# The seven products of each pair of tiles of the branch projections, pair by pair

## The chip, the cores and the metric

The kernel runs on one core of one Trainium2 chip. The metric is device microseconds (us) of one execution, as the median of three timed runs. One more execution was taken with the hardware profiler; its rows are what this document reads. Engines in these rows: PE is TensorE's matmul, PEld its weight load, DVE is VectorE, ACT is ScalarE, POOL is GpSimd, and SP is SyncE, whose queue (SPq) issues the DMA transfers here.

## The reference

One inference step of a decoder layer (DEPTH is 1) on 1024 prompt rows and 8 single samples, D_MODEL 1024, branch width 512, all in fp32. The part that the change touches is the merge of three branches by gates:

```python
h = _rmsnorm(x, norm_g) * (1 + scale) + shift
p = h @ w_in
...                                     # y_a, y_b, y_c: three branches, each (T, 512)
merged = (jax.nn.sigmoid(m_a) * (y_a @ w_branch[0])
          + jax.nn.sigmoid(m_b) * (y_b @ w_branch[1])
          + jax.nn.sigmoid(m_c) * (y_c @ w_branch[2]))
x = x + gate * (merged @ w_out)
```

`w_branch[b]` is 512 x 1024. So each branch projection is a product of 1024 x 512 weights with 512 x 1032 data, multiplied element by element by a gate and added to the other two.

## The kernel before

**Data.** Data lie transposed: features on the 128 partitions, the 1032 columns (1024 rows and 8 samples) along the free axis, in two halves of H = 516, each in two parts of HC = 258 columns, which is the width of a matmul. A fp32 product is made of three matmuls on numbers split in a high and a low part: high weights by high data (L1120), high weights by low data (L1121), low weights by high data (L1122). The split of a block is two instructions: ScalarE makes the high part (L109), VectorE the low one as the difference (L110). High parts have names with h (`yh0T4`), low ones with l (`yl0T4`).

**Seven products a pair.** The projection of a branch has eight tiles of 128 output features. Two tiles `m0`, `m1` form a pair and are computed together by a scheme with seven block products in place of eight (a variant of Strassen's): the weights come as A11, A12, A22 (in `pw..a`, high and low half) and sums S1 to S4 (in `pw..s`), the data as blocks B11, B21, B22 and sums T1 to T4. The sums of the weights were made earlier and lie in HBM, as do the gates (`sd`, after ScalarE's sigmoid, stored by L991 and L992) and the branches (`yd`). A product is 12 matmuls of 128x258 (two parts of columns, two blocks of 128 rows, three matmuls each). Branches come in the order 1, 0, 2 (`n` = 0, 1, 2), four pairs each: p10 to p13, p00 to p03, p20 to p23. The list `flat` holds these 12 pairs. The seven products of a pair, and what follows each:

```python
"P1": J(mm("B1", "A11", "B11", True, False), seed, dma, a=WD),
"P5": J(mm("B5", "S1", "T1", True, False), snap("B5", "p5")),
"P2": J(mm("B2", "A12", "B21", False, True), lambda: gated(m0, 0, "B2"), s_dma, r=-1.0, a=SD),
"P6": J(mm("B1", "S2", "T2", False, False), snap("B1", "u2")),
"P3": J(mm("B5", "S4", "B22", False, True), right, r=0.0),
"P7": J(mm("B1", "S3", "T3", False, False), lambda: added(m1, "B1", "p5", False), r=0.0),
"P4": J(mm("B1", "A22", "T4", False, True), last, r=-1.0),
```

P1 writes bank B1. The *seed* (ScalarE, L1140) copies B1 to bank B2, where P2 adds its product; P6, P7 and P4 add theirs to B1. The *snaps* (ScalarE, L1134) copy P5's bank and, after P6, B1 to an array `pu`. VectorE adds P3's bank to one half of `pu` and multiplies by the gate of m0 (`right`: L1150 twice, L1153), after P7 the same for m1; *gated* (L1145, two instructions) multiplies P2's bank by m0's gate, and P4's by m1's. So the first half of columns of m0 comes from P2, that of m1 from P4. After P4, `summed` (L1159) adds m0 and m1 to the sums of the branches before (for n of 1 and 2).

**The planner.** Each product is a `Job`; the jobs run in the order in which they were made, and this fixes the order of instructions on every engine. A job's `dma` goes out as soon as the job is nearer than its lead, counted in the planned durations (1.45 us for a product) of the jobs between: WD = 16 us for the weights of a pair (at P1, L1099), SD = 8 us for its two gates (at P2, L1104). Within that, transfers are issued on SyncE in the order of the jobs that triggered them, between whatever else SyncE has to issue, and SyncE's queue takes its rows one after the other. Work that may come later is put in a list `behind` (`later`), and each job takes from it: a product with positive room (P1, P5, P6: 1.0) right after its matmuls and ahead of its own copies, one with negative room (P2, P4: -1.0) behind its own, and P3 and P7 take none. The splits of the *next* branch's blocks, and the sums T1 to T4 (L1062) that they need, are put in that list by the table NEXT: the entry `(3, "P6"): "T4"` says that when P6 of the branch's last pair (number 3) is made, the split of T4 for the next branch goes on the list. `"dma"` loads the next branch's data (L1056, eight transfers, `yr`).

**The order.** `go` makes one product's job. Each pair runs P5, P2, P6, P3, P7, then P1 of the *next* pair, then its own P4; the very last pair has P5, P6, P3, P7, P2, P4.

Of the kernel before, what the change touches and what calls it, by code (L numbers as in the profile page):

```python
# [56 lines left out]

RM = 1.0

NEXT = {(1, "P2"): "dma", (1, "P4"): "B11", (1, "P3"): "T1+", (2, "P5"): "T1", (2, "P2"): "B21 T3+", (2, "P6"): "T2+ T4+",  # L60
        (3, "P5"): "T2 B22", (3, "P2"): "T3", (3, "P6"): "T4"}

LAST = {(1, 2): "dma", (1, 4): "B11", (1, 5): "T1+", (1, 6): "T1", (0, 0): "B21", (0, 1): "T3+", (0, 2): "T2+", (0, 3): "T4+",
        (0, 4): "T2", (0, 5): "B22", (0, 6): "T3", (0, 7): "T4"}
# [10 lines left out]
def hybrid_step_kernel(ctx: ExitStack, tc: tile.TileContext, ins, outs):  # L75
# [1177 lines left out]
    flat = [(n, i, t) for n in range(3) for i, t in enumerate(branches[n])]  # L1253

    def go(j, x):
        n, i, t = flat[j]
        t[x]()
        if n < 2 and (i, x) in NEXT:
            hooks[n + 1](NEXT[i, x])

    go(0, "P1")
    for j in range(len(flat)):
        for x in ("P5", "P2", "P6", "P3", "P7") if j + 1 < len(flat) else ("P5", "P6", "P3", "P7", "P2"):
            go(j, x)
        if j + 1 < len(flat):
            go(j + 1, "P1")
        go(j, "P4")


    wo_h, wo_l, xr, oacc = {}, {}, {}, {}  # L1270
# [265 lines left out]
```

## Time and profile before

| | |
|---|---|
| median of 3 runs | 903.98 us (903.88 to 906.06) |
| the profiled execution | 906.72 us, of which the span (first to last instruction) is 905.0 us |
| granted TensorE clock, mean of the span | 0.995 of full speed |
| TensorE busy | 890.9 us, 98% |
| VectorE, ScalarE, GpSimd busy | 625.0, 398.5, 30.4 us |
| moved by DMA | 152.96 MB, 169 GB/s on average |

The sum of what happens is set by the engine that is always busy, here TensorE. A busy share is an average over the program's stages: the stretch that this change touches runs from about 674.8 us (first product of p10) to 797.1 us (end of p23), and is read by itself below. The rows give a start and a duration in us, the engine, the line, and what was written from what; "idle before <-" names what an engine waited for. A line number is that of the kernel before.

### The profile page before, as it was taken

The page shows a single profiled execution, that of the slowest core. Times are in us where ns is not written, and L with a number is a line of the kernel's source. Part 1 is how long each engine was busy: PE and PEld are TensorE (multiplying, and loading weights), DVE is VectorE, ACT ScalarE, POOL GpSimd, SP SyncE. Part 2 cuts the span into 40 slices and gives each one's busy share as a digit, 9 for nine tenths or more (in the row PEclk, how much of TensorE's full clock was granted, in tenths as well). Part 3 has the DMA queues.
Part 4 walks back from the last instruction along what each step waited for, and adds up shares of the span by engine and source line. Part 5 has one row for each costly group of instructions (what it writes and reads, how often), then busy time and mean ns, then how long its engine had stood idle before and what let it go on. Part 6 is the DMA issues. An engine that isn't in the chain of part 4 may idle for free.

```text
span 905.0 us, 17515 instructions
## 1 busy us (share of the span) xinstructions
PE 890.9 (98%) x7126; PEld 864.2 (95%) x7126; DVE 625.0 (69%) x1149; ACT 398.5 (44%) x743; POOL 30.4 (3%) x72
## 2 busy tenths in 40 slices
PE   8999999999999999999999999999999999999996
PEld 8677999999999999999999999999999999999995
DVE  4676758667877667866756667578565889893634
ACT  5666572454444334335544544445453433451211
POOL 1450000000000000000000000000000000000001
PEclk9999999999999999999999999999999999999998
DMA  8905213225746263440721614606579999570103
GB/s 314 353 1 152 76 67 86 83 90 211 255 166 231 94 221 117 177 152 13 281 82 71 245 47 141 222 1 234 188 276 388 385 338 347 206 255 1 49 23 118
DMA packets 65185, 152.96 MB, mean 169 GB/s; under 512 B 12232, under 2 KB 23240, under 8 KB 65104
## 3 DMA queue, kind: packets, MB, share of 16 engines
q1 hardware_dynamic: 65104, 151.83, 47.0%
q8 instruction: 56, 0.92, 0.4%
q14 instruction: 25, 0.20, 0.1%
HBM read 105.95 MB, written 45.86 MB: 168 GB/s over the span
## 4 chain that ended last, share of the span: by engine, by line
PE 90%; DVE 1%; ACT 1%; issue 0%; DVEq 0%
PE o L1287 3%; PE o L1288 3%; PE o L1289 3%; PE g_2B L575 2%; PE g_1B L577 2%; PE g_2B L577 2%; PE g_0B L577 2%; PE g_3B L577 2%; PE g_0B L578 2%; PE g_2B L578 2%; PE g_1B L575 2%; PE g_0B L575 2%; PE g_1B L578 2%; PE g_3B L578 2%; PE g_3B L575 2%; PE u0B L575 1%
## 5 line engine op out<-in xcount | busy, mean ns | idle before, releaser
L1287 PE MATMUL o<-mh,woh 128*128 128x388 f32 (+1 forms) x192 | 62.2, 324 | 0.0
L1288 PE MATMUL o<-ml,woh 128*128 128x388 f32 (+1 forms) x192 | 61.5, 320 | 0.0
L1289 PE MATMUL o<-mh,wol 128*128 128x388 f32 (+1 forms) x192 | 61.3, 319 | 0.0
L1288 PEld LDWEIGHTS o<-ml,woh 128*128 128x128 f32 x192 | 36.1, 188 | 0.3
L1287 PEld LDWEIGHTS o<-mh,woh 128*128 128x128 f32 x192 | 36.1, 188 | 0.3
L1289 PEld LDWEIGHTS o<-mh,wol 128*128 128x128 f32 x192 | 36.2, 188 | 0.0
L1391 ACT ACTIVATE osq<-xr 128x388 f32<-128x388 f32 (+1 forms) x21 | 10.3, 492 | 48.5 <-DVE xr L1380 28.1
L375 PE MATMUL v<-bvw,hhi 128*128 128x512 f32 x64 | 26.4, 413 | 0.2 <-ACT hhi L292 0.2
L377 PE MATMUL v<-bvw,hlo 128*128 128x512 f32 x64 | 25.5, 398 | 0.7 <-DVE hlo L296 0.7
L376 PE MATMUL v<-bvw,hhi 128*128 128x512 f32 x64 | 25.2, 394 | 0.0
L1377 DVE SCALAR_TENSOR_TENSOR xr<-o,gt,xr 128x384 f32<-128x384 f32 x16 | 9.8, 614 | 19.9 <-PE o L1289 19.8
L323 PE MATMUL warm<-ones 128*128 128x128 f32 x158 | 21.4, 300 | 1.1 <-DVE ones L130 1.1
L323 PEld LDWEIGHTS warm<-ones 128*128 128x128 f32 x158 | 20.6, 214 | 1.9 <-DVE ones L130 1.1
L577 PE MATMUL g_1B<-hlo,g_1wB 128*128 128x258 f32 x72 | 20.4, 283 | 0.0
L575 PE MATMUL g_1B<-hhi,g_1wB 128*128 128x258 f32 x72 | 20.4, 283 | 0.0
L575 PE MATMUL g_2B<-t,g_2w 128*128 128x258 f32 x72 | 20.4, 283 | 0.0
L575 PE MATMUL g_2B<-hhi,g_2wB 128*128 128x258 f32 x72 | 20.4, 283 | 0.0
L577 PE MATMUL g_2B<-hlo,g_2wB 128*128 128x258 f32 x72 | 20.4, 283 | 0.0
L577 PE MATMUL g_1B<-t,g_1w 128*128 128x258 f32 x72 | 20.4, 283 | 0.0
L578 PE MATMUL g_1B<-hhi,g_1wB 128*128 128x258 f32 x72 | 20.4, 283 | 0.0
L578 PE MATMUL g_0B<-hhi,g_0wB 128*128 128x258 f32 x72 | 20.4, 283 | 0.0
L578 PE MATMUL g_2B<-hhi,g_2wB 128*128 128x258 f32 x72 | 20.3, 283 | 0.0
(1393 smaller groups left out, 3741.4 us busy)
## 6 DMA issues: line engine op xcount, KB each, us to landing
sig<-sd SPq DMA_DIRECT2D x24, 516.0 KB, 6.5
ada<-in_ada SPq DMA_DIRECT2D x16, 512.0 KB, 8.4
wr<-in_wbr SPq DMA_DIRECT2D x12, 512.0 KB, 5.0
x<-in_xT SPq DMA_DIRECT2D x16, 256.0 KB, 6.2
gr<-in_ada_g SPq DMA_DIRECT2D x8, 512.0 KB, 7.1
wor<-in_wo SPq DMA_DIRECT2D x8, 512.0 KB, 4.9
xr<-in_xf SPq DMA_DIRECT2D x8, 512.0 KB, 5.3
sd<-g_0o SPq DMA_DIRECT2D x6, 516.0 KB, 3.3
```

The costliest lines, as they stand in the source:

```text
L323: PE.matmul(ps[:, :P], lhsT=ones, rhs=ones, start=True, stop=True)
L375: PE.matmul(vacc[i], lhsT=lh, rhs=w[:, 0, :], start=start, stop=False)
L376: PE.matmul(vacc[i], lhsT=lh, rhs=w[:, 1, :], start=False, stop=False)
L377: PE.matmul(vacc[i], lhsT=ll, rhs=w[:, 0, :], start=False, stop=stop)
L575: PE.matmul(o, lhsT=w[:, 0, f_], rhs=bh, start=start and k == 0, stop=False, skip_group_check=True)
L577: PE.matmul(o, lhsT=w[:, 0, f_], rhs=bl, start=False, stop=False, skip_group_check=True)
L578: PE.matmul(o, lhsT=w[:, 1, f_], rhs=bh, start=False, stop=stop and k == KW - 1, skip_group_check=True)
L1287: PE.matmul(o, lhsT=wo_h[k][:, w], rhs=cols(mhi[k]), start=start, stop=False)
L1288: PE.matmul(o, lhsT=wo_h[k][:, w], rhs=cols(mlo[k]), start=False, stop=False)
L1289: PE.matmul(o, lhsT=wo_l[k][:, w], rhs=cols(mhi[k]), start=False, stop=stop)
L1377: V.scalar_tensor_tensor(x[:, :m], ps[:, :m], gt[:, f, 0:1], x[:, :m], ALU.mult, ALU.add)
L1391: A_.activation(o_like(c, sq), x, AF.Square)
```

## The change

Every pair now runs its own seven products P1, P5, P6, P3, P7, P2, P4, in the order that only the last pair ran in nearly the same form before. No product of the next pair comes ahead of P4, and P2 comes as last but one. The table NEXT is written anew with the same tasks in the same order, hooked to the products that now stand in the places: for instance the split of T4 goes on the list at (3, "P2"), which is now the sixth product of the pair.

```diff
-NEXT = {(1, "P2"): "dma", (1, "P4"): "B11", (1, "P3"): "T1+", (2, "P5"): "T1", (2, "P2"): "B21 T3+", (2, "P6"): "T2+ T4+",
-        (3, "P5"): "T2 B22", (3, "P2"): "T3", (3, "P6"): "T4"}
+NEXT = {(1, "P6"): "dma", (1, "P2"): "B11", (1, "P4"): "T1+", (2, "P5"): "T1", (2, "P6"): "B21 T3+", (2, "P2"): "T2+ T4+",
+        (3, "P5"): "T2 B22", (3, "P6"): "T3", (3, "P2"): "T4"}
...
-    go(0, "P1")
     for j in range(len(flat)):
-        for x in ("P5", "P2", "P6", "P3", "P7") if j + 1 < len(flat) else ("P5", "P6", "P3", "P7", "P2"):
+        for x in ("P1", "P5", "P6", "P3", "P7", "P2", "P4"):
             go(j, x)
-        if j + 1 < len(flat):
-            go(j + 1, "P1")
-        go(j, "P4")
```

What stands in a row on two engines, before and after. First SyncE's queue around the first pair, p10, before: `pw10s1` and `pw11..` are weights of the pairs p10 and p11, `sig1_0` and `sig1_1` the gates of p10's two tiles, `sd2_6` and `sd2_7` the stores of the last two gate tiles that the stage before computes.

```order
L1099 DMA pw10s1_7872<-wd10s1_2183 128x1024
L1104 DMA sig1_0_8001<-sd1_0_777 128x1032
L1104 DMA sig1_1_8003<-sd1_1_778 128x1032
L1099 DMA pw11a0_8005<-wd11a0_2445 128x768
L1099 DMA pw11a1_8007<-wd11a1_2447 128x768
L1099 DMA pw11s0_8009<-wd11s0_2435 128x1024
L1099 DMA pw11s1_8011<-wd11s1_2437 128x1024
L991 DMA sd2_6_791<-g2_3o1_7937 128x1032
L992 DMA sd2_7_792<-g2_3o2_7968 128x1032
L1104 DMA sig1_2_8118<-sd1_2_779 128x1032
```

And the same place of SyncE's queue after the change:

```order
L1099 DMA pw10s1_7872<-wd10s1_2183 128x1024
L991 DMA sd2_6_791<-g2_3o1_7937 128x1032
L992 DMA sd2_7_792<-g2_3o2_7968 128x1032
L1104 DMA sig1_0_8035<-sd1_0_777 128x1032
L1104 DMA sig1_1_8037<-sd1_1_778 128x1032
L1099 DMA pw11a0_8039<-wd11a0_2445 128x768
L1099 DMA pw11a1_8041<-wd11a1_2447 128x768
L1099 DMA pw11s0_8043<-wd11s0_2435 128x1024
L1099 DMA pw11s1_8045<-wd11s1_2437 128x1024
L1056 DMA yr0B11_8180<-yd0_0_757 128x516
```

The two stores moved from behind six loads to ahead of them, and the next branch's data (`yr0`) now come right behind `pw11`.

Second, VectorE in the first pair of a following branch, p00, before. `p00B2`, `p00B5` and `p00B1` are the banks (the last digit is the part of columns), `yl0..` the low parts of the blocks of this branch.

```order
L110 TENSOR_TENSOR yl0B22_8597<-yr0B22_8193,yh0B22_8596 128x1032
L1145 TENSOR_TENSOR sig0_0_8504<-p00B20_8560,sig0_0_8504 128x258
L1145 TENSOR_TENSOR sig0_0_8504<-p00B21_8562,sig0_0_8504 128x258
L110 TENSOR_TENSOR yl0T3_8618<-yr0B12_8190,yh0T3_8617 128x1032
L110 TENSOR_TENSOR yl0T4_8634<-yr0B21_8187,yh0T4_8633 128x1032
L1150 TENSOR_TENSOR p00pu_8600<-p00B50_8582,p00pu_8600 128x258
L1150 TENSOR_TENSOR p00pu_8600<-p00B51_8589,p00pu_8600 128x258
L1153 TENSOR_TENSOR sig0_0_8504<-p00pu_8600,sig0_0_8504 128x516
L1150 TENSOR_TENSOR p00pu_8600<-p00B10_8546,p00pu_8600 128x258
L1150 TENSOR_TENSOR p00pu_8600<-p00B11_8553,p00pu_8600 128x258
L1153 TENSOR_TENSOR sig0_1_8506<-p00pu_8600,sig0_1_8506 128x516
L1145 TENSOR_TENSOR sig0_1_8506<-p00B10_8546,sig0_1_8506 128x258
```

The same pair on VectorE after the change:

```order
L110 TENSOR_TENSOR yl0B22_8597<-yr0B22_8189,yh0B22_8596 128x1032
L110 TENSOR_TENSOR yl0T3_8616<-yr0B12_8186,yh0T3_8615 128x1032
L1150 TENSOR_TENSOR p00pu_8600<-p00B50_8582,p00pu_8600 128x258
L1150 TENSOR_TENSOR p00pu_8600<-p00B51_8589,p00pu_8600 128x258
L1153 TENSOR_TENSOR sig0_0_8548<-p00pu_8600,sig0_0_8548 128x516
L1150 TENSOR_TENSOR p00pu_8600<-p00B10_8560,p00pu_8600 128x258
L1150 TENSOR_TENSOR p00pu_8600<-p00B11_8567,p00pu_8600 128x258
L1153 TENSOR_TENSOR sig0_1_8550<-p00pu_8600,sig0_1_8550 128x516
L1145 TENSOR_TENSOR sig0_0_8548<-p00B20_8578,sig0_0_8548 128x258
L1145 TENSOR_TENSOR sig0_0_8548<-p00B21_8580,sig0_0_8548 128x258
L110 TENSOR_TENSOR yl0T4_8666<-yr0B21_8183,yh0T4_8665 128x1032
L1145 TENSOR_TENSOR sig0_1_8550<-p00B10_8560,sig0_1_8550 128x258
```

P2's two multiplications moved from the second place to the last but one, and the low part of T4 moved with them, from ahead of the pair's sums to between P2's multiplications and P4's.

Third, VectorE from the last pair of branch 0, p03, to the first of branch 2, p20, after the change: `sig1_4` and `sig1_5` are the running sums of finished tiles.

```order
L1145 TENSOR_TENSOR sig0_6_8951<-p03B20_8978,sig0_6_8951 128x258
L1145 TENSOR_TENSOR sig0_6_8951<-p03B21_8980,sig0_6_8951 128x258
L1159 TENSOR_TENSOR sig1_4_8297<-sig1_4_8297,sig0_4_8820 128x1032
L1145 TENSOR_TENSOR sig0_7_8953<-p03B10_8963,sig0_7_8953 128x258
L1145 TENSOR_TENSOR sig0_7_8953<-p03B11_8970,sig0_7_8953 128x258
L1159 TENSOR_TENSOR sig1_5_8299<-sig1_5_8299,sig0_5_8822 128x1032
L110 TENSOR_TENSOR yl2T2_9102<-yr2B11_8701,yh2T2_9101 128x1032
L110 TENSOR_TENSOR yl2B22_9124<-yr2B22_8710,yh2B22_9123 128x1032
L110 TENSOR_TENSOR yl2T3_9143<-yr2B12_8707,yh2T3_9142 128x1032
```

Before, P2's multiplications and the sum of `sig1_4` stood ahead of the pair's own additions (L1150, L1153), and only the sum of `sig1_5` and P4's multiplications came between those and the split of T2; now two sums and four multiplications stand in a row ahead of that split.

## Rows read from the trace of the kernel before

**Rows 1.** The head of the page and its first section: the span; for each engine the time in which it was busy, its share of the span, and the number of its instructions.

```profile
span 905.0 us, 17515 instructions
...
PE 890.9 (98%) x7126; PEld 864.2 (95%) x7126; DVE 625.0 (69%) x1149; ACT 398.5 (44%) x743; POOL 30.4 (3%) x72
```

**Rows 2.** The list of TensorE's waits: the waiting instruction's tile and line, what it waited for, then the sum in us, how often, and the longest.

```profile
PE ss L204 <- DVE sq L228: 2.2, 1, 2.2
...
PE p23B L1120 <- DVE p23pu L1150: 0.5, 1, 0.5
PE p10B L1120 <- ACT p10B L1140: 0.3, 1, 0.3
```

**Rows 3.** TensorE's timeline: start and duration in us, then the operation, its tile and its inputs, and idle time before it where there was any (the first matmul of P2 in p10 after the seed; the first matmuls of P1, P5's low weights, P2 in p11; the first of p12; and the first two of P4's data T4, here named with its blocks, in p23). The last row is of the view of one tile, `pw12s`: least, median and largest duration in ns, then the start of the first and of the last of 12.

```profile
678.17 0.39 PE L1120 MATMUL p10B<-yh1B,pw10a 128*128 128x258 f32 x1 [0.33 <-ACT p10B L1140]
...
684.06 0.29 PE L1120 MATMUL p11B<-yh1B,pw11a 128*128 128x258 f32 x1
...
687.17 0.28 PE L1122 MATMUL p11B<-yh1T,pw11s 128*128 128x258 f32 x1
...
688.36 0.28 PE L1120 MATMUL p11B<-yh1B,pw11a 128*128 128x258 f32 x1
...
694.12 0.28 PE L1120 MATMUL p12B<-yh1B,pw12a 128*128 128x258 f32 x1
...
795.56 0.39 PE L1120 MATMUL p23B<-yh2T,pw23a 128*128 128x258 f32 x1 [0.53 <-DVE p23pu L1150]
795.79 0.28 PE L1121 MATMUL p23B<-yl2T,pw23a 128*128 128x258 f32 x1
...
L1122 PE MATMUL p12B<-yh1T,pw12s x12: 279/284/289, 697.2 to 704.1; 128*128 128x258 f32 x12
```

**Rows 4.** SyncE's queue from 663 us on (start and length of the issuing, a row for neighbours of one kind); then the issuing of pw12s by itself; then, for one transfer each, the size and the time from its issue to its landing (the sig issued at about 677.8 and the second pw12s at 687.5); then SyncE's wait for the stores of the last gates; and ScalarE's row that the first of these stores waits for.

```profile
663.23 0.80 SPq L1104 DMA_DIRECT2D sig<-sd  x2
664.08 2.69 SPq L1099 DMA_DIRECT2D pw11a<-wd11a  x2
666.86 1.70 SPq L1099 DMA_DIRECT2D pw11s<-wd11s  x2
676.92 0.32 SPq L991 DMA_DIRECT2D sd<-g_3o  x1
...
677.81 1.98 SPq L1104 DMA_DIRECT2D sig<-sd  x2
...
L1099 SPq DMA_DIRECT2D pw12s<-wd12s x2: 319/320/320, 686.8 to 687.5; - x2
...
sig<-sd SPq DMA_DIRECT2D x1, 516.0 KB, 5.5
...
pw12s<-wd12s SPq DMA_DIRECT2D x1, 512.0 KB, 8.1
...
SPq L991 <- ACT g_3o L990: 16.0, 3, 8.3
...
675.83 1.06 ACT L990 ACTIVATE g_3o<-g_3o 128x1032 f32<-128x1032 f32 x1
```

**Rows 5.** Stretches of the core: start and end in us, length, busy time (and instructions) of PE, PEld, DVE, ACT and POOL, TensorE's granted clock as a share of full speed, the share of the 16 DMA engines' time that transfers took, and GB/s.

```profile
670.00:677.00 7.00, 7.00 (x61) 7.00 (x61) 3.90 (x7) 2.36 (x5) 0.00 (x0) 1.00 0.51 204
677.00:682.00 5.00, 4.67 (x39) 4.47 (x38) 3.13 (x4) 3.70 (x8) 0.00 (x0) 1.00 0.89 307
682.00:687.00 5.00, 5.00 (x44) 5.00 (x43) 3.34 (x7) 0.74 (x2) 0.00 (x0) 1.00 0.99 359
687.00:692.00 5.00, 5.00 (x44) 5.00 (x44) 1.28 (x3) 1.54 (x4) 0.00 (x0) 1.00 1.04 400
692.00:697.00 5.00, 5.00 (x45) 5.00 (x44) 4.40 (x8) 0.74 (x2) 0.00 (x0) 1.00 1.03 418
697.00:702.00 5.00, 5.00 (x44) 5.00 (x43) 2.76 (x5) 3.42 (x7) 0.00 (x0) 1.00 1.03 409
```

**Rows 6.** VectorE's timeline (start, duration, operation, idle before): a multiplication of L1145 after P2 in p11, one by a gate of 516 columns, sums of L1062 and L1159 and multiplications back to back between p03 and p20, splits there, the second multiplication of P2 in p22 with the next row, and the additions in p23. Then three rows of ScalarE: the two halves of the seed in p11, and the high part of a split.

```profile
690.00 0.43 DVE L1145 TENSOR_TENSOR sig<-p11B,sig 128x258 f32<-128x258 f32 x1 [0.29 <-PE p11B L1122]
...
693.41 0.70 DVE L1153 TENSOR_TENSOR sig<-p11pu,sig 128x516 f32<-128x516 f32 x1
...
752.18 1.22 DVE L1159 TENSOR_TENSOR sig<-sig,sig 128x1032 f32<-128x1032 f32 x1
753.33 0.75 DVE L1150 TENSOR_TENSOR p03pu<-p03B,p03pu 128x258 f32<-128x258 f32 x2
...
758.05 1.23 DVE L110 TENSOR_TENSOR yl2T<-yr2B,yh2T 128x1032 fp32r<-128x1032 f32 x1
...
760.33 0.75 DVE L1145 TENSOR_TENSOR sig<-p20B,sig 128x258 f32<-128x258 f32 x2
761.00 2.37 DVE L110 TENSOR_TENSOR yl2T<-yr2B,yh2T 128x1032 fp32r<-128x1032 f32 x2
...
787.89 0.43 DVE L1145 TENSOR_TENSOR sig<-p22B,sig 128x258 f32<-128x258 f32 x1 [0.29 <-PE p22B L1122]
788.24 1.22 DVE L1159 TENSOR_TENSOR sig<-sig,sig 128x1032 f32<-128x1032 f32 x1
...
795.09 0.75 DVE L1150 TENSOR_TENSOR p23pu<-p23B,p23pu 128x258 f32<-128x258 f32 x2
...
684.97 0.37 ACT L1140 ACTIVATE p11B<-p11B 128x258 f32<-128x258 f32 x1 [3.21 <-PE p11B L1122]
685.70 0.37 ACT L1140 ACTIVATE p11B<-p11B 128x258 f32<-128x258 f32 x1 [0.35 <-PE p11B L1122]
...
717.18 1.06 ACT L109 ACTIVATE yh0B<-yr0B 128x1032 fp32r<-128x1032 f32 x1
```

**Rows 7.** Two stretches near the start of the program, with the columns of rows 5.

```profile
20.00:24.00 4.00, 3.96 (x42) 2.89 (x42) 2.17 (x8) 0.27 (x1) 0.00 (x0) 0.78 1.03 414
24.00:28.00 4.00, 4.00 (x25) 3.18 (x21) 2.94 (x9) 1.19 (x3) 0.23 (x1) 0.80 1.03 409
```

## The prediction

> **What bounds the kernel now.** I read the page first. TensorE (PE) is busy for 890.9 of 905.0 us [rows 1], so what counts is whether TensorE waits, and the list of waits [rows 2] names its few waits. The longest, 2.2 us, is at the start of the program. In the stretch that the change touches, from about 674.8 to 797.1 us, there are two: one product of pair p10 waits for ScalarE's copy (the seed), and the last product of pair p23 waits for VectorE. The timeline of TensorE [rows 3] gives the pace: from the first product of p11 (684.06) to the first of p12 (694.12) seven products pass in 10.06 us, 1.437 us for one of 12 matmuls, 0.12 us for a matmul. Nothing is left to gain but those two waits, about 0.33 + 0.53 us. The question is what the new order makes late.
>
> Then I read the queue that issues transfers [rows 4] and the load on the DMA engines [rows 5]. SyncE's queue issues in row order. The loads of the first pair's gates (sig) and of p11's weights (pw11a, pw11s) go out between 663.2 and 668.6, and the queue then stands until 676.92, held by the store of the last gate tile, which waits for ScalarE's L990 (675.83 plus 1.06 us). From 677 on the engines are full: 307, 359, 400, 418, 409 GB/s in five windows of 5 us, at a share of 0.89 to 1.04. Before, from 670 to 677, the share is 0.51. So the transfers, hidden until now, are the second resource that is full.
>
> **The change part by part.** No instruction is added or removed; 7 products of 12 matmuls for each of 12 pairs stay, and so does their pace. Three moves matter.
>
> *The loads.* The planner gives the gates' loads to the second product, 8 us ahead of it, and the weights' loads to the first, 16 us ahead of it. Both products now come later, and the order on SyncE shows the result: the store of the last gate tile now stands ahead of sig1_0, sig1_1 and the four loads of pw11. All six, 2 x 0.528 + 2 x 0.393 + 2 x 0.524 = 2.89 MB, move from an open stretch (663 to 674) behind 676.92, where the engines are already full. In the new order the bytes from 676.92 on add up, in MB, to: two stores 1.06, both sig 2.11, pw11a 2.90, pw11s 3.95, the eight yr0 6.06, sig1_2 6.59, sig1_3 7.12, pw12a 7.90, pw12s 8.95. The engines' own curve [rows 5] has moved 1.54 MB by 682, 3.33 by 687, 5.33 by 692, 7.42 by 697, and 0.409 MB a us from there. A transfer lands later than its last byte by this curve: the third in the queue (sig, at 677.81 plus 5.5) lands at 683.3 where the curve has it at 682.1, and the second pw12s (687.5 plus 8.1) lands at 695.6 where the curve says 693.75 [rows 4, 5]. I take 1.5 us between these 1.2 and 1.85.
>
> Now each against its need, with TensorE's rows as the clock (position by position the products of the new order start at the same times as the old ones until something waits). The first product of p11 would start at 684.06 + 1.44 = 685.50 and needs the low half of pw11a with its third matmul, at 685.74; it lands at 685.8 + 1.5 = 687.3: late by 1.6. The second product needs the low half of pw11s at 687.17 [rows 3]; it lands at 688.5 + 1.5 = 690.0: late by 2.8 in all. The last product of p11 (694.12) needs VectorE to have read the bank that it writes to, and in VectorE's queue that read stands behind the multiplication by sig1_2 (0.70 us and 0.43 us for the two, [rows 6]), so sig1_2 is needed by 693.0 and lands at 695.0 + 1.5: 3.5 in all. pw12a is needed at 695.8 and lands at 698.2 + 1.5: 3.9. pw12s is needed at 697.2 [rows 3] and lands at 700.75 + 1.5 = 702.25: 5.0 in all. After that the queue gains on TensorE: a pair takes 10.06 us and its loads are 2.89 MB, 7.1 us at 0.409. pw13s lands at about 709.3 and is needed at 707.2 + 5.0. So the loads cost **5.0 us**. Bounds: at 0.418 MB a us from 677.6 and a lag of 1.2 us pw12s lands at 700.3, late by 3.1; if the whole 2.89 MB shifts what landed at 695.6 at 0.400, it lands at 702.8, late by 5.6. A gain is excluded: no transfer starts earlier than before.
>
> The Trainium skill weighs on this: "DMA: Bandwidth & Descriptors", section Bandwidth, says that between HBM and SBUF the HBM side binds, at about 358 GB/s for a core. By that figure the 5.62 MB left at 687 would take 15.7 us instead of 13.75, pw12s would land 1.95 us later, an estimate, and the loads would cost 7.0. The windows here show 400 to 418 GB/s for 15 us, so I keep to them.
>
> *T4, the last block of the next branch.* Its split used to be put off to the fourth product of the last pair, and VectorE's row of it stood ahead of p00's sums. Now it is put off to the sixth product (P2) of the last pair of the branch before, and the order on VectorE has it in p00 behind P2's two multiplications, right ahead of P4, which needs it. From P2's first matmul to VectorE's second multiplication: 688.36 to 690.00, 1.64 us [rows 3, 6]. The next instruction on VectorE starts 0.35 us later (787.89 to 788.24), the split takes 1.22, and TensorE starts 0.05 us after VectorE ends (795.09 + 0.42 against 795.56): 3.26 us. P4's second matmul, the first that reads the low half, would come at 1.44 + 0.12 = 1.56. TensorE waits 1.70, and its next matmul comes 0.23 instead of 0.12 us later [rows 3]: 1.8 us in p00 and the same in p20, **3.6 us**. Nothing hides it, since P4 is followed by nothing of the next pair any more, and TensorE takes its rows in order.
>
> *T2 in p20.* There VectorE also adds up two finished tiles between the pairs. From P2 of p03: multiplication 1.64 + 0.35, a sum 1.14, two multiplications 0.67, a sum 1.14, the split of T2 1.23 [rows 6]: 6.17 us. P6 of p20 reads it at 4 x 1.437 + 0.12 = 5.87. Late by 0.3 plus 0.05 and 0.1: **0.45 us**. In p00, without sums, it is there 1.2 us early (P4's second multiplication ends at 1.44 + 1.64 + 0.43, T2 about 1.1 later). B22 and T3 come just in time: ScalarE splits each in 1.06 us [rows 6] between its other copies and VectorE follows with 1.22; by the same addition B22 is 0.1 to 0.2 us ahead of its matmul and T3 about 0.1. I cost them at nothing, at most 0.2 us for each branch.
>
> *The seed and the snaps.* P6 follows P1 after one product and must wait until the seed has read the bank. In p11 the seed's second half ends at 686.07, 2.0 us after P1's first matmul [rows 3, 6]; P6 comes at 2 x 1.437 = 2.87, so P5 covers it. In p10 the seed is late today (0.33 us of idle at 678.17), and P6 takes over that wait from P2: no change. Of p23 the rows are the same, so its 0.53 us stays.
>
> **The sum.** 5.0 + 3.6 + 0.45 = 9.05 us. The profiled execution lasted 906.7 us (span 905.0 and 1.7 around it) and would last 915.8. It stood 2.7 above the median of the three timed runs, 903.98; there I expect 903.98 + 9.05 = **913.0 us**. Differences under 0.3% (2.7 us) count as no change throughout, about what a measurement of this kernel can tell.
>
> **The rivals.**
> - *The loads come in time and only VectorE's order costs.* 4.05 us, 908.0. It needs 8.95 MB landed by 697.2, that is 494 GB/s from 677.6 on; no window shows over 418 [rows 5]. For it speaks that landing is inferred from a queue with another mix. Chance 0.17.
> - *TensorE's clock falls in the new waits.* After the 2.2 us wait at the start, granted clock 0.78 and 0.80 stands over 20 to 28 us [rows 7]: part of it at the lower of the two levels (1.2 of 2.4 GHz), 1.7 us lost. New waits of 1 to 1.8 us stand at p11, p12, p00, p20. With two falls 3.4 us more: 916.4. Against it: the waits of 0.33 and 0.53 us left the clock at 1.00 in every window from 677 [rows 5]. Chance 0.20. The Trainium skill, "TensorE: Matmul & The Clock Gate", Part 1, says that idling throttles the clock to half rate; the row agrees, and by that rule this rival would happen if waits this long count as idling.
> - *The queues' order does not bind.* If SyncE let ready loads pass the waiting store and VectorE took T4 when ScalarE is done, nothing would be late, and the two waits of today could vanish: 903.98 - 0.9 = 903.1, not slower. It decides at the store (loads out before about 670) and at T4. Against it: sig at 677.81 stood behind the store at 676.92 though the engines were free, and VectorE's p23pu at 795.09 came behind other rows while TensorE waited. Chance 0.04.
> - The forecast itself: 0.58; 0.01 is left for a gain that I do not see.
>
> **How the numbers follow.** Slower by over 0.3% are the forecast and the first two rivals, 0.95; within 0.3% the third, 0.04; faster 0.01. The loads' bounds (3.1 to 5.6) put the forecast itself at 911.1 to 913.6. For 8 in 10 the range reaches down to the first rival, 907.6, and up past the clock's, 917.0.
>
> **What the profile would show.** Right: TensorE waiting for DMA in p11 and p12 (pw11a, pw11s, pw12a, pw12s), or on p11pu behind a VectorE that waits for sig; a wait of about 1.7 us for VectorE's yl0T and yl2T in p00 and p20; sig and pw11 issued after 677.7. Wrong: pw11s landing before 687, or p00's P4 without a wait. The forecast fails most likely in the size of the loads' delay.

## The result, and the profile after

The median of four executions is 914.61 us after the change (913.81 to 917.87) and 904.27 us before (903.88 to 906.06). The ratio is 1.0111, with a 95% interval of 1.0093 to 1.0129: slower by about 10 us, where 9.05 had been forecast (913.0, range 907.6 to 917.0).

The total time of one profiled execution is a blunt measure here. The start of the program differs from run to run: TensorE's wait at L204 is 2.2 us before [rows 2], 2.7 after, 0.6 in one of the runs below and absent in another. So this text compares profiles by one stretch, from the first matmul of p10 to the first matmul of the output projection (`o`), which holds all that the change touches. Before, it runs from 674.83 to 797.11, 122.28 us. After, by TensorE's timeline:

```profile
676.36 0.28 PE L1120 MATMUL p10B<-yh1B,pw10a 128*128 128x258 f32 x1
...
808.47 0.33 PE L1283 MATMUL o<-mh,woh 128*128 128x388 f32 x1
```

That is 132.11 us, longer by **9.83**. The 1.53 us by which p10 begins later (676.36 against 674.83) come from the program's start and are no part of it. TensorE's list of waits after (compare [rows 2]; columns as there):

```profile
PE p11B L1120 <- DVE p11pu L1150: 2.0, 1, 2.0
PE p20B L1121 <- DVE yl2T L110: 1.8, 2, 1.5
PE p00B L1121 <- DVE yl0T L110: 1.5, 1, 1.5
...
PE p11B L1122 <- DMA pw11s<-wd11s: 0.7, 1, 0.7
```

VectorE's timeline has the row that the first of these waits hangs on, the multiplication by sig1_2 in p11:

```profile
698.72 0.70 DVE L1153 TENSOR_TENSOR sig<-p11pu,sig 128x516 f32<-128x516 f32 x1 [3.28 <-DMA sig<-sd]
```

All these new waits are at places that the prediction named (p20's two are listed together). The longest names VectorE, but VectorE itself had stood for 3.28 us before it, waiting for the gate's transfer, so that wait is really one for a transfer. SyncE's queue shows why (compare [rows 4]):

```profile
678.45 0.32 SPq L991 DMA_DIRECT2D sd<-g_3o  x1
678.82 0.42 SPq L992 DMA_DIRECT2D sd<-g_3o  x1
679.29 2.01 SPq L1104 DMA_DIRECT2D sig<-sd  x2
681.35 0.96 SPq L1099 DMA_DIRECT2D pw11a<-wd11a  x2
682.40 0.97 SPq L1099 DMA_DIRECT2D pw11s<-wd11s  x2
683.47 7.39 SPq L1056 DMA_DIRECT2D yr0B<-yd  x8
691.27 0.97 SPq L1104 DMA_DIRECT2D sig<-sd  x2
692.61 1.00 SPq L1099 DMA_DIRECT2D pw12a<-wd12a  x2
695.34 1.00 SPq L1099 DMA_DIRECT2D pw12s<-wd12s  x2
```

The gates and the weights of p11, issued from 663 to 669 before, now go out from 679 to 683, behind the store, and everything after them is late too. The stretches show what that did to the DMA engines and to TensorE's clock (columns of [rows 5]):

```profile
670.00:677.00 7.00, 7.00 (x61) 7.00 (x61) 5.44 (x9) 2.29 (x5) 0.00 (x0) 1.00 0.01 2
...
687.00:692.00 5.00, 4.15 (x32) 3.69 (x31) 1.29 (x4) 1.13 (x3) 0.00 (x0) 1.00 1.03 409
692.00:697.00 5.00, 5.00 (x44) 5.00 (x43) 0.85 (x2) 2.12 (x4) 0.00 (x0) 1.00 1.05 398
697.00:702.00 5.00, 2.99 (x19) 2.78 (x18) 3.07 (x7) 0.00 (x0) 0.00 (x0) 0.85 1.03 418
702.00:707.00 5.00, 5.00 (x37) 5.00 (x36) 2.71 (x3) 1.88 (x5) 0.00 (x0) 0.81 1.03 409
```

From 670 to 677, where the engines were busy for half of the time before, they now stand idle (2 GB/s), and from 687 they are full. TensorE does less work in the windows from 687 and from 697 (4.15 and 2.99 of 5 us), and after the wait of 2.0 us the granted clock falls to 0.85 and 0.81, part of the time at the lower of the two levels.

Measured at the last matmul of each pair (and 1.44 us taken off the rows of before, where the next pair's first product has by then been made), the delay is 5.7 us up to p13, 1.9 us in p00, 2.3 us in p20 and nothing elsewhere: 9.8 us together before rounding.

### The profile page after: what moved, and what is told of

Read it like the earlier page. It is cut to its first block, busy times and chain, and to the rows that moved or that the text cites. A ratio compares the mean times of both kernels' runs of the same rounds, so it can differ in the third digit from the quotient of the medians.

```text
span 916.1 us, 17512 instructions
## 1 busy us (share of the span) xinstructions
PE 895.3 (98%) x7126; PEld 866.9 (95%) x7126; DVE 625.3 (68%) x1149; ACT 398.3 (43%) x743; POOL 30.3 (3%) x72
## 4 chain that ended last, share of the span: by engine, by line
PE 86%; DVE 2%; DMA 2%; ACT 1%; issue 0%; DVEq 0%; SPq 0%
PE o L1283 3%; PE o L1284 3%; PE o L1285 3%; PE g_2B L575 2%; PE g_1B L577 2%; PE g_2B L577 2%; PE g_0B L577 2%; PE g_3B L577 2%; PE g_0B L578 2%; PE g_2B L578 2%; PE g_0B L575 2%; PE g_1B L578 2%; PE g_1B L575 2%; PE g_3B L578 2%; PE g_3B L575 2%; PE u0B L575 1%
## 5 line engine op out<-in xcount | busy, mean ns | idle before, releaser
L1387 ACT ACTIVATE osq<-xr 128x388 f32<-128x388 f32 (+1 forms) x21 | 10.3, 491 | 48.3 <-DVE xr L1376 28.0
```

Of the source, the lines that this page charges most:

```text
L1387: A_.activation(o_like(c, sq), x, AF.Square)
```

## The experiments

Eight more kernels were run, 4 to 12 executions each, in two sessions in which the median of the kernel before was 905.91 us (the first four) and 905.55 us (the last four); this is the neighbour in what follows. The table puts their ratios beside their stretches (p10's first matmul, the first matmul of `o`, the length, and its difference to 122.28):

| kernel | ratio to before, 95% | p10 | `o` | stretch | difference |
|---|---|---|---|---|---|
| the change | 1.0111 (1.0093 to 1.0129) | 676.36 | 808.47 | 132.11 | +9.8 |
| gates earlier | 1.0049 (1.0036 to 1.0062) | 674.90 | 801.47 | 126.57 | +4.3 |
| T4 earlier | 1.0087 (1.0074 to 1.0100) | 672.49 | 802.88 | 130.39 | +8.1 |
| both | 1.0036 (1.0023 to 1.0049) | 671.82 | 796.77 | 124.95 | +2.7 |
| gates before yr0 | 1.0124 (1.0108 to 1.0140) | 673.05 | 805.12 | 132.07 | +9.8 |
| old order, late loads | 1.0077 (1.0054 to 1.0100) | 678.74 | 807.00 | 128.26 | +6.0 |
| next P1 in between | 1.0015 (0.9997 to 1.0032) | 676.94 | 801.00 | 124.06 | +1.8 |
| P2 second | 1.0077 (1.0054 to 1.0100) | 672.65 | 802.00 | 129.35 | +7.1 |
| T4 earlier in two pairs | 1.0007 (0.9988 to 1.0026) | 678.65 | 802.04 | 123.39 | +1.1 |

### Gates earlier: the loads put back

```diff
-WD, SD = 16.0, 8.0
+WD, SD = 16.0, 12.0
```

> The change, with one number put back: the lead of the gates' loads is 12 us instead of 8, so that SyncE issues sig1_0, sig1_1 and the weights of p11 ahead of the last gate tile's store again, as before the change. Theory (loads late in SyncE's queue, and apart from that VectorE's order): no wait for pw11a, pw11s or in p11's last product, granted clock 1.00 from 690 to 710; the waits for yl0T4 in p00 and yl2T2, yl2T4 in p20 stay (1.9 and 2.3 us of delay in the trace after the change), so about 904.3 + 4.4 = 908.7 us. Rival (the new order of products itself makes p11 wait, whatever the loads do): p11's last product waits 2 us as before this edit and the time stays at 914.

910.41 us, 4.5 above its neighbour. TensorE's list of waits has only VectorE's splits left (beside those of before and of the program's start):

```profile
PE p20B L1121 <- DVE yl2T L110: 1.7, 2, 1.5
PE p00B L1121 <- DVE yl0T L110: 1.5, 1, 1.5
```

By its stretches the clock stands at 1.00 where it fell after the change:

```profile
690.00:700.00 10.00, 10.00 (x86) 10.00 (x86) 6.73 (x12) 3.24 (x7) 0.00 (x0) 1.00 1.03 415
700.00:710.00 10.00, 10.00 (x86) 10.00 (x85) 8.64 (x14) 4.19 (x8) 0.00 (x0) 1.00 1.03 407
```

So the loads' place in the queue, above all that of the six ahead of the store, is worth 5.5 us of stretch, and p11's waits have nothing to do with the order of products as such. From 690 on the DMA engines are just as full as after the change (415 and 407 GB/s); the difference is that from 670 to 677 they moved 223 GB/s here, and 2 GB/s after the change.

### T4 earlier: VectorE's order

```diff
-                "P3": J(mm("B5", "S4", "B22", False, True), right, r=0.0),
+                "P3": J(mm("B5", "S4", "B22", False, True), right, r=-1.0),
```

> The change, with the third-from-last place for put-off work opened: after P3's additions one piece of put-off work is taken, so that VectorE splits T2, B22, T3 and T4 one place earlier and T4's low part stands ahead of the first pair's additions. The loads stay late. Theory: the waits in p00 (yl0T) and p20 (yl2T) vanish, 1.9 + 2.3 us; the waits in p11 and the clock's fall stay: 914.6 - 4.2 = 910.4 us. Rival (the waits for yl0T and yl2T are an effect of TensorE running after its stall in p11, or the piece of work only moves the wait to P7's additions): 913 to 915.

913.86 us, 7.95 above its neighbour, where 6.1 had been expected. The waits for yl0T and yl2T did vanish, but the open place let VectorE take other put-off work too (sums of finished tiles), and P7's additions came late in two pairs, as the second half of the rival had it. The loads' waits stayed, and a third of their kind appeared. TensorE's waits:

```profile
PE p11B L1120 <- DVE p11pu L1150: 1.9, 1, 1.9
...
PE p03B L1120 <- DVE p03pu L1150: 0.9, 1, 0.9
...
PE p11B L1122 <- DMA pw11s<-wd11s: 0.7, 1, 0.7
PE p12B L1122 <- DMA pw12s<-wd12s: 0.7, 1, 0.7
...
PE p20B L1120 <- DVE p20pu L1150: 0.7, 1, 0.7
```

Up to p13 this kernel and the change are late by the same 5.8 and 5.7 us, although here the clock stayed at 1.00 (next fence) after a wait of 1.93 us. In its place stands the wait for pw12s: after the change, where the clock fell, TensorE came to pw12s later, and found it there. TensorE's stretches of this run:

```profile
690.00:695.00 5.00, 3.94 (x33) 3.73 (x32) 1.07 (x3) 0.99 (x2) 0.00 (x0) 1.00 1.03 406
695.00:700.00 5.00, 3.75 (x26) 3.29 (x26) 4.97 (x10) 0.74 (x2) 0.00 (x0) 1.00 1.03 421
700.00:705.00 5.00, 4.61 (x38) 4.61 (x39) 1.04 (x3) 2.78 (x6) 0.00 (x0) 1.00 1.03 409
```

### Both

The two edits above together.

> Both edits of the two runs beside it: gates' loads 12 us ahead, one piece of put-off work taken after P3. Theory: if the queue of loads and VectorE's order are the whole of the loss, the pairs run one by one as fast as before, TensorE waits only in p10 (seed, 0.3) and p23 (0.5): 904 to 905 us, within 0.3% of the kernel before. Rival (running pair by pair has a price in every pair, from seeds, snaps or VectorE's reads of the banks): 12 pairs with 0.2 to 0.4 us each, 907 to 909.

908.36 us, 2.45 above its neighbour: not the 0 to 1 of the theory. The time lies in the rival's 907 to 909, but there is no price in every pair: the new waits are the two of 0.9 and 0.7 us that the open place after P3 makes, in p03 and p20, and p12 and p02 last 0.2 us longer. VectorE's timeline of p03 shows how:

```profile
750.91 0.70 DVE L1153 TENSOR_TENSOR sig<-p03pu,sig 128x516 f32<-128x516 f32 x1
751.53 1.23 DVE L1159 TENSOR_TENSOR sig<-sig,sig 128x1032 f32<-128x1032 f32 x1
752.67 0.75 DVE L1150 TENSOR_TENSOR p03pu<-p03B,p03pu 128x258 f32<-128x258 f32 x2
```

A sum of 1.14 us stands between P3's multiplication and P7's additions, and P4 waits for the latter.

### Gates before yr0: is it one load, or the queue?

```diff
-NEXT = {(1, "P6"): "dma", (1, "P2"): "B11", (1, "P4"): "T1+", ...
+NEXT = {(1, "P2"): "dma", (1, "P4"): "B11", (2, "P1"): "T1+", ...
```

> The change, with the next branch's data (yr0, 2.1 MB) hooked to the sixth product of p11 instead of the second on, so that SyncE issues sig1_2 and sig1_3 ahead of them; the bytes ahead of pw12s are the same. Theory (the amount that is queued ahead of pw12s sets p12's start; the clock's fall only filled time that pw12 would have cost): p11's wait for sig1_2 vanishes and p12 waits for pw12a and pw12s instead, the same end within 1 us: 913.6 to 915. Rival (the late sig1_2 and the clock's fall that follows it are the cost): 2.2 us and 1.6 us gone, 910.5 to 911.5.

The stretch is 132.07 us, that of the change 132.11, and the ratios' intervals overlap. By time this kernel is at 917.64 us, above the 913.6 to 915 expected: the profiled execution took 914.57 us at a mean granted clock of 0.997, the other three 916.95 to 919.19 at 0.989 to 0.993. Where their clock was low is not shown, so the comparison rests on the stretch. The longest wait of the change, for sig1_2, is gone, and the clock does not fall from 690 on; TensorE now waits in p12, by its timeline:

```profile
697.39 0.39 PE L1120 MATMUL p12B<-yh1B,pw12a 128*128 128x258 f32 x1 [0.69 <-DMA pw12a<-wd12a]
698.32 0.39 PE L1122 MATMUL p12B<-yh1B,pw12a 128*128 128x258 f32 x1 [0.43 <-DMA pw12a<-wd12a]
...
700.88 0.39 PE L1122 MATMUL p12B<-yh1T,pw12s 128*128 128x258 f32 x1 [0.70 <-DMA pw12s<-wd12s]
```

So neither the wait for sig1_2 nor the clock's fall behind it is what the change costs. The bytes queued ahead of pw12s set when p12 can go on, and the waits that come before only fill that time.

### Old order, late loads

The kernel before, with

```diff
-WD, SD = 16.0, 8.0
+WD, SD = 16.0, 5.0
```

> The kernel before, with one number changed: the gates' lead 5 us instead of 8, so that SyncE issues the last gate tile's stores ahead of sig1_0, sig1_1 and the weights of p11, as the change does; the order of the products and of VectorE's splits is that of before. Theory: the late loads alone cost what the stretch after the change lost up to p13, 5.5 to 5.8 us (p12's weights land at the same time, and the second product of p12 stands in the same place in both orders), 1.0062 to 1.0066 of the time of before; TensorE waits for pw11a, pw11s, pw12a and pw12s. Rival (the old order, with a product of the next pair in between, covers part of it): 2 to 3.5 us.

The stretch grew by 6.0 us, 5.9 of them up to p13. The median is 913.60 us, 8.05 above its neighbour; by the ratio of 1.0077 it is 7 us, with an interval of 4.9 to 9.1. TensorE waited for pw11a and pw12a, as expected, but not for pw11s and pw12s, which had landed by the time that it came to them. Its waits, and its stretch behind the first of them:

```profile
PE p11B L1120 <- DMA pw11a<-wd11a: 1.4, 1, 1.4
PE p12B L1120 <- DMA pw12a<-wd12a: 1.2, 1, 1.2
...
690.00:695.00 5.00, 4.59 (x26) 4.51 (x26) 1.19 (x3) 0.74 (x2) 0.00 (x0) 0.66 1.03 419
```

The expected size came by another transfer than the expected one. In the old order P1 of p12 stands a product earlier and needs pw12a that much earlier, and P4 of p11 stands between it and the product that needs pw12s. So the last wait is for pw12a here and for pw12s in the kernel with the gates before yr0, and both come to about the same 5.5 to 5.9 us up to p13: late loads cost the same in either order of products. The granted clock fell here too, to 0.66 from 690 to 695; TensorE still had to wait for pw12a afterwards.

### Next P1 in between

```diff
+    go(0, "P1")
     for j in range(len(flat)):
-        for x in ("P1", "P5", "P6", "P3", "P7", "P2", "P4"):
+        for x in ("P5", "P6", "P3", "P7", "P2"):
             go(j, x)
+        if j + 1 < len(flat):
+            go(j + 1, "P1")
+        go(j, "P4")
```

The gates' lead is 12 us here and in the last kernel; P2 second, between them, kept the 8 us of before.

> The change with the gates' lead at 12 us (the loads go out in time), and with the next pair's first product put back between P2 and P4; P2 stays last but one, and so does T4's split behind P2's multiplications. Theory: the product in between covers 1.44 us of the wait for T4's low part, so that p00 and p20 lose about 0.4 us each to it and 0.2 each to T2, in all 1.0 to 1.4 us above the kernel before, where the run with the gates' lead alone lost 4.3. Rival (P2's late place is what costs, whatever stands between): 4 us and more.

1.4 us above its neighbour by time (interval -0.3 to 2.9) and 1.8 by stretch, 0.8 in each of p00 and p20: a little over the expected 0.6. In p00 the idle time ahead of P4's low part is 0.26 us by these two rows of TensorE (0.38 between starts in place of 0.12), where the change has 1.70:

```profile
728.44 0.28 PE L1120 MATMUL p00B<-yh0T,pw00a 128*128 128x258 f32 x1
728.82 0.39 PE L1121 MATMUL p00B<-yl0T,pw00a 128*128 128x258 f32 x1
```

One product between P2 and P4 is the cover that the change took away.

### P2 second: the other half of the change alone

```diff
-        for x in ("P1", "P5", "P6", "P3", "P7", "P2", "P4"):
+        for x in ("P1", "P5", "P2", "P6", "P3", "P7", "P4"):
```

with the table NEXT of before. The gates' lead is the 8 us of before, not the 12 that the expectation names.

> The other half alone: each pair by itself in the order P1, P5, P2, P6, P3, P7, P4, P2 in its old place, with the table NEXT of before and the gates' lead at 12 us. Theory: P4 now follows P7 at once, and writes to the bank that VectorE must still read for P7's additions, behind P3's additions and multiplication. By rows of before VectorE starts P7's addition about 0.6 us after P3's second one ends up, so that TensorE would wait 0.4 to 0.5 us in each of 11 pairs: 4.5 to 5.5 us above the kernel before, in small waits for pu in every pair, and no wait for T4. Rival (VectorE is off the path there): within 1 us of the kernel before.

913.97 us, 8.4 above its neighbour (7 us by the ratio of 1.0077, interval 4.9 to 9.1), and 7.1 by stretch, where 4.5 to 5.5 had been expected. Each pair lasts 10.56 us in place of 10.08, as expected, and the last product of every pair waits for pu; here p11's, and p23's:

```profile
692.84 0.39 PE L1120 MATMUL p11B<-yh1T,pw11a 128*128 128x258 f32 x1 [0.22 <-DVE p11pu L1150]
...
800.46 0.38 PE L1120 MATMUL p23B<-yh2T,pw23a 128*128 128x258 f32 x1 [2.14 <-DVE p23pu L1150]
```

The 0.48 us of a pair is more than the 0.22 in the row: in p11 the starts lie 0.50 apart at this wait (692.34 to 692.84) and 0.23 after it, in place of 0.12 each. What was not expected is p23: there VectorE splits for the output projection (L110, `wol` and `ml`) ahead of the additions, the second `wol` only after 2.37 us of waiting for ScalarE, and without P2 between P7 and P4 the wait of 0.53 us [rows 3] becomes 2.14. Behind it, and after the end of the stretch, the granted clock fell (0.50 from 802 to 804). So P4 needs some product between P7 and itself, whichever it is: the next pair's first (before) or P2 (the change). The run shows one thing more: with P2 in its old place SyncE issued the gates and p11's weights from 661 to 666, ahead of the store at 674.74, at a lead of 8 us. So it is P2's late place that put the loads behind the store, and not the running of each pair by itself.

### T4 earlier in two pairs

```diff
-                "P3": J(mm("B5", "S4", "B22", False, True), right, r=0.0),
+                "P3": J(mm("B5", "S4", "B22", False, True), right, r=-1.0 if n and i == 0 else 0.0),
```

> The change with the gates' lead at 12 us and the place for put-off work after P3 opened in p00 and p20 alone, where T4 needs it. Theory: the waits of 0.9 us in p03 and 0.7 us in p20 that the open place caused in every pair fall away, those for T4 stay away, and 0.2 to 0.3 us for T2 in p20 and as much for P7's additions in p00 remain: 0.3 to 1 us above the kernel before, no difference that can be measured. Rival (T4's split behind P3's additions holds back P7's additions by its whole 1.14 us in both pairs): 2 to 2.5 us above.

905.80 against 905.55 us, ratio 1.0007 (0.9988 to 1.0026): no difference to the kernel before that can be measured. Once the loads and T4's split are put right, running pair by pair costs little by itself: 1.1 us of stretch are left, 0.3 in p00 and 0.7 in p20. TensorE's waits in the stretch:

```profile
PE p23B L1120 <- DVE p23pu L1150: 0.5, 1, 0.5
PE p10B L1120 <- ACT p10B L1140: 0.3, 1, 0.3
PE p20B L1121 <- DVE yl2T L110: 0.2, 1, 0.2
```

No version was faster than the kernel before. The only waits left in its stretch are the 0.33 and 0.53 us of [rows 3], less than these runs could show.

## Why the prediction was right, point by point

**TensorE as the bound, and its pace.** Right: pairs without a new wait last about 10.08 us in every kernel but P2 second, and the stretch moved with TensorE's waits.

**The loads.** The mechanism was right and is shown from both sides: the loads put back take 5.5 us away, the loads made late in the old order add 6.0. The size was 5.0 forecast and 5.7 measured, just past the upper bound of 5.6. The term that was mis-sized is the lag of 1.5 us between the last byte by the curve and the landing, taken as the same for all. Turned back to the clock of before (1.53 us off), pw11a let TensorE go on at 688.04 - 1.53 = 686.5 where 687.3 was forecast, pw11s at 690.56 - 1.53 = 689.0 (forecast 690.0), but sig1_2 let VectorE start at 698.72 - 1.53 = 697.2 (forecast 696.5), and pw12s let TensorE go on at 700.88 - 673.05 + 674.83 = 702.7 in the run with the gates before yr0 (forecast 702.25). The lag grew from about 0.6 us at the queue's head to 2 us at its end; why it grows is not shown. It is not a slower rate: in windows 1.53 us later the engines moved 297, 385, 402 and 403 GB/s after the change, where those of before have 302, 359, 400 and 418. After the change itself TensorE shows no wait for pw12s. Its second half, issued at 696.02, landed 8.3 us later, at 704.3:

```profile
pw12s<-wd12s SPq DMA_DIRECT2D x1, 512.0 KB, 8.3
```

TensorE came to it at 704.54, held up by the slow clock. So of the 0.7 us that the loads cost beyond the forecast, about 0.5 is the lag, and about 0.2 the clock's fall. Two small delays were missed as well: sig1_0 holds back VectorE in p10 too (0.5 us by the start of p11), which costs nothing more, because p12's weights set the end; and each restart after a wait costs another 0.1 us, which the prediction counted for T4 and T2 but not here.

The stretches after show 398 to 418 GB/s for 20 us from 687 on. The Trainium skill, "DMA: Bandwidth & Descriptors", section Bandwidth, would have put the limit between HBM and SBUF at about 358 GB/s for a core; the measured rate stands, and the loads' 5.7 us are nearer to 5.0 than to the 7.0 by that figure. Two figures of the prediction do not follow as written: its lower bound comes to 3.0 by its own terms, not 3.1, and the 494 GB/s has the lag of 1.5 us taken off without saying so (457 without it). Neither changes an argument, as no window of [rows 5] shows over 418.

**T4.** Right: 1.8 us forecast for p00, 1.9 measured. TensorE's timeline after:

```profile
731.66 0.28 PE L1120 MATMUL p00B<-yh0T,pw00a 128*128 128x258 f32 x1
733.48 0.40 PE L1121 MATMUL p00B<-yl0T,pw00a 128*128 128x258 f32 x1 [1.54 <-DVE yl0T L110]
733.71 0.29 PE L1122 MATMUL p00B<-yh0T,pw00a 128*128 128x258 f32 x1
```

1.82 us between two matmuls in place of 0.12: a stall of 1.70, as the sum had it, and 0.23 in place of 0.12 to the next.

**T2 in p20.** Right: 2.25 us forecast for p20 together with T4, 2.3 measured; the wait for yl2T at P6 is 0.23 us by the trace, and 0.39 by the starts.

**Seed and snaps.** Right: p10's wait for the seed only changed its product (0.32 us), and no other pair waits for ScalarE.

**The rivals.** "Only VectorE's order costs" (0.17) fell: the loads were late. "The queues' order does not bind" (0.04) fell with it. "TensorE's clock falls" (0.20) came half true: it fell once, in p11 and p12, but its price was the mistake. The prediction added the lost time to the sum, 1.7 us for a fall. In this place it costs about 0.2 us, since TensorE would have waited for pw12s in most of that time; the kernels with T4 earlier and with the gates before yr0 kept the clock at 1.00 there and came to the end of p13 within 0.2 us of the change. When a wait is followed by a fall is not settled: waits of 2.01 us (the change), 1.44 us (the old order with late loads, with one of 0.41 us right behind it) and 2.14 us (P2 second) were, and one of 1.93 us at the same place as the first, behind nearly the same work, was not, nor those of 1.54 us in p00 and p20. The Trainium skill, "TensorE: Matmul & The Clock Gate", Part 1, has idling throttle the clock; the three falls agree with that, and the waits without a fall leave open which idling counts. The prediction's argument against a fall holds up to 702 by [rows 5]; the wait of 0.53 us came at 795, where those rows do not reach, but the trace of before has 1.00 there too (792 to 802).

**The sum.** 9.05 forecast, 9.83 by stretch and 10.3 by the medians. Of the 0.8 by which the stretch is longer, 0.7 is in the loads, and 0.1 in p00 and p20.

## What to carry to other kernels

When a job is moved in a program whose planner issues transfers by leads, look first at which transfers fall behind a waiting instruction of their queue: six loads that slipped behind one store cost 5.7 us here, VectorE's order 4.2. Where one late queue feeds several waits in a row, the last one sets the time: here taking away an earlier wait, or the slow clock between them, gave back no more than 0.2 us. A product of other work between a result and its reader is cover: the order can do without the next pair's product, but only where the splits and loads are moved to fit.

## What the runs showed of the hardware

How far a transfer landed behind the engines' curve of before grew along a full queue, from 0.6 to about 2 us. TensorE's granted clock fell behind waits of 1.44, 2.01 and 2.14 us and stayed at 1.00 behind others of 1.54 and 1.93. The start of the program varied by itself: TensorE's wait at L204 was from under 0.6 to 2.7 us, and the granted clock from 10 to 40 us was 0.77 in the kernel with late loads in the old order:

```profile
10.00:40.00 30.00, 27.78 (x196) 21.42 (x195) 18.58 (x33) 15.26 (x24) 3.70 (x9) 0.77 1.04 408
```

and 1.00 in that with P2 second, though the program is the same in both up to there, so that only the execution differs; this is why total times of single executions say less than the stretch:

```profile
10.00:40.00 30.00, 28.88 (x242) 22.23 (x241) 21.80 (x38) 18.18 (x28) 7.59 (x14) 1.00 1.04 408
```
